# Eight more read buffers in the activations' memory, norm columns read one stage earlier, and another order at the ends of the expert layers

## The chip, the core and the metric

The kernel runs on one core of a Trainium2 chip. The core has five engines that run side by side, each through its own instructions in order: PE (matmuls), DVE (VectorE, element-wise work on 128 partitions), ACT (ScalarE, functions of one input), POOL (GpSimd) and SP, which here only issues transfers. Transfers from the chip's main memory (HBM) to the on-chip memory (SBUF) are asynchronous: an engine issues one, and 16 DMA engines carry it out. Plain reads are issued by SP, reads of rows by an index list (gathers) by POOL. The metric is the time of one execution in microseconds (us); it is the median of several.

## The reference

Two layers, 256 tokens of width 1024, all in float32. With `ada = c @ w_ada + b_ada` split into sh1, sc1, g1, sh2, sc2, g2, each layer computes

```
h      = rmsnorm(x, norm1_g) * (1 + sc1) + sh1
q, k, v, b_gate, c_gate, hc, gate_a, gate_c = split(h @ w_in)
ya     = causal attention(q, k, v) with a distance penalty, 8 heads
yc     = b_gate * short_conv(c_gate * hc)
merged = sigmoid(gate_a) * (ya @ w_attn_proj) + sigmoid(gate_c) * (yc @ w_conv_proj)
x      = x + g1 * (merged @ w_out)
h      = rmsnorm(x, norm2_g) * (1 + sc2) + sh2
q      = h @ w_query; per token and head: top 16 of 128 x 128 pairs of keys, softmax gates
x      = x + g2 * sum over the 8 x 16 chosen experts of gate * gelu(h . expert_u[i]) * expert_v[i]
```

and at the end `rmsnorm(x, final_g)`. There are 16,384 experts in a layer, so expert_u and expert_v have 67 MB each.

## The kernel before

**One stream of reads.** All large weights are read once, in the order of a list named `stream`, in groups of 1 MB (two units of 128 x 1024 floats). `load_ahead` issues the next group on SP as soon as a buffer is free: there are three (`NRAW`) of 8 KB per partition in the pool `strm`, and five others that serve only the first 13 groups. SP issues in order, so a group that waits for a buffer holds up all later ones. `weave(main, extra, spots)` puts extra groups between the weights at given positions. The extra groups are the columns of `ada` (`ada_pair`: a shift and a scale for 128 channels, reduced on DVE in `ada_unit`, line 255) and its rows for the gates (`ada_rows`, line 252).

**Mixer** (the first half of a layer: norm, attention, convolution, gates, output). Its weights are split in a high part (`wh`, ACT, line 305) and a low part (`wl`, DVE or POOL, line 310), and PE multiplies three times. `pol["pool"]` is the share of the low parts that goes to POOL: `POOL_MIX` in most of the mixer, 0.34 in the projections and the output. `unit` prepares units some two to four ahead of the one that PE takes. 16 extra groups go between the weights: eight pairs of columns for the second norm and eight pairs of rows for g1 and g2.

**Expert half.** The two tiles of 128 tokens are treated differently. Tile 0 is *dense*: PE multiplies it with all of expert_u (128 units of 128 experts, line 1052), ACT applies gelu into `halves` (`al` and `ah`, 64 x 128 floats each per partition, the activations), the activations are multiplied by the routing weights that PE builds from one-hot factors (`weigh`, lines 1023 to 1041), and PE multiplies them with all of expert_v (line 1106). Tile 1 is *gathered*: for each of its 128 (head, rank) slots, POOL issues a gather of the 128 chosen rows of expert_u (0.5 MB) and DVE takes a dot product (line 962); the same for expert_v, where DVE adds the scaled row (line 970). So a layer has 128 gathers of each. `NROWS` = 7 gathers can be in flight; `use` consumes the oldest and issues the next.

The order of all this is written out by hand. In the query projection (`query`) scores are handed to `route_all`, a chain of DVE work for the top-k that runs in the background: `fill` takes some of it per step. In the loop over U, each expert unit is followed by one `fill` while routing lasts, or by steps of `weigh` from expert 64 on, and one `use`. In the loop over V, `use` is paced so that the gathers are used up by unit 118 of 128. At unit 122 the update of the gathered tile's `x` is emitted, and after the loop that of the dense tile. In layer 0, eight pairs of columns for layer 1's first norm are woven evenly into U and V. `experts` opens the memory of `al` and `ah` only after the query projection; before that it is the mixer's.

Of the kernel before, what the change touches and what calls it, by code (L numbers as in the profile page):

```python
# [8 lines left out]
F32 = mybir.dt.float32  # L9
# [16 lines left out]
NE = 128  # L26
NROWS = 7
# [5 lines left out]
SPOTS = [int((i + 0.5) * 19 / 16) for i in range(16)]  # L33
# [5 lines left out]
POOL_START, POOL_MIX, POOL_PROJ = 0.5, (0.45, 0.3), 0.34  # L39
# [7 lines left out]
def body(ctx: ExitStack, tc: tile.TileContext, d: dict, out: bass.AP):  # L47
# [60 lines left out]
    for l in range(DEPTH):  # L108
        n = NFIRST[l]
        pairs("qk", d["w_qk"][l, :n], n)  # L110
        pairs("v", d["w_v"][l], 4)
        pairs("qk", d["w_qk"][l, n:], 8 - n)
        pairs("conv", d["w_cv"][l], 12)
        pairs("gate", d["w_gt"][l], 16)
        for u in range(4):
            groups.append(("proj", [(slice(0, 1), d["w_ap"][l][u:u + 1].rearrange("u p c -> p u c")),
                                    (slice(1, 2), d["w_cp"][l][u:u + 1].rearrange("u p c -> p u c"))]))
        a = take_groups()
        ex = [ada_rows(l, r, k) for r in range(2) for k in range(0, KD, 2)]
        if l == 0:  # L120
            cols = [ada_pair(0, 0, m) for m in range(KD)]
            parts = {"c": cols, "u": a[:n // 2], "v": a[n // 2:n // 2 + 2]}
            a = a[n // 2 + 2:]
            start = [parts[ch].pop(0) for ch in START]
            assert not any(parts.values())
            ex = [ada_pair(0, 2, m) for m in range(KD)] + ex
            a = start + weave(a, ex, SPOTS)
        else:
            ex = [ada_pair(l, 2, m) for m in range(KD)] + ex
            a = weave(a, ex, [4 + int(i * 20 / 16) for i in range(16)])  # L130
        stream += a
        pairs("out", d["w_out"][l].rearrange("(k p) c -> k p c", p=128), 8)
# [12 lines left out]
    raws = {}  # L145

# [3 lines left out]
    def load_ahead():  # L150

        while state["dma"] < len(stream):
            kind, parts = stream[state["dma"]]
            if state["dma"] < len(START):
# [166 lines left out]
    def dense_done():  # L321
        raws.pop(state["unit"] // 2)
        state["unit"] += 2
        state["out"] -= 1
        load_ahead()
# [587 lines left out]
    def experts(es, xp, l, hf, pss):  # L913
# [9 lines left out]
        rp = es.enter_context(tc.tile_pool(name="route", bufs=1, side="right"))  # L923
# [86 lines left out]
        ah = es.enter_context(tc.tile_pool(name="acth", bufs=1, side="right")).tile([128, 64, 128], F32, name="ah")  # L1010
        low = ExitStack()
        al = low.enter_context(tc.tile_pool(name="actl", bufs=1, side="right")).tile([128, 64, 128], F32, name="al")
        halves = (al, ah)
# [32 lines left out]
        for e in range(0, NE, 4):  # L1046
# [19 lines left out]
            A.activation(halves[e // 64][:, e % 64:e % 64 + 4], ps, AF.Gelu_apprx_tanh)  # L1066
        for _ in weighing:
            pass
# [6 lines left out]
        for e in range(0, NE, 2):  # L1075
# [14 lines left out]
            if e == 122:  # L1090
                assert not flying and not tasks
                warm_sqrt()
                xg = None
                if fg is not None:
                    xg = tail.tile([128, NT, D], F32, name="xg"), fg
                update(tail, ys, row, 1, xg, 0)
                if xg:
                    z, ops = rstd_ops(1, 2)
                    for op in ops:
                        op()  # L1100
                    scale(xg[0], 1, z, V, A)
            raw = dense("V")
            for x in range(2):
# [6 lines left out]
                while len(tasks) + len(flying) > left * (1 - (i + 1) / 118):  # L1110
# [5 lines left out]
        if xg:  # L1116
            y, ops = rstd_ops(0, 1)
            update(tail, ys, row, 0, xg, 0)
            for op in ops:
                op()  # L1120
            scale(xg[0], 0, y, V, A)
            es.close()
            return None
        pol["pool"] = 1.0
        while len(ready) < 2 and next_unit():
            pass
        update(tail, ys, row, 0, None, 0)
        xps = turn_x((1, 0))
# [12 lines left out]
    for l in range(DEPTH):  # L1141
# [13 lines left out]
        xps = experts(es, xp, l, hf, norm_full(l, xps, hf))  # L1155
# [67 lines left out]
```

## Time and profile before

| | |
|---|---|
| median of 3 runs | 1918.09 us (1917.17 to 1921.28) |
| the profiled execution | 1917.63 us |
| its span, first to last instruction | 1915.8 us |
| busy: PE, DVE | 1637.6 us (85%), 1418.7 us (74%) |
| busy: POOL, ACT | 709.9 us (37%), 572.1 us (30%) |
| moved by transfers | 669.22 MB, 349 GB/s over the span |

The shares are averages over stages with different limits; what holds in one stage is seen only when the span is cut into stages. A busy PE in such a table can still have small gaps, since the ends of matmuls are modelled.

### The profile page before, as it was taken

The numbers are of one execution on the slowest core, as the hardware profiler recorded it, in microseconds if no ns is written. First come the engines' busy times: TensorE is split into PE (matmuls) and PEld (weight loads), VectorE is DVE, ScalarE is ACT, GpSimd is POOL, SyncE is SP. The second block draws the span as 40 slices with busy tenths as digits, with TensorE's granted clock in tenths as the row PEclk, the third lists the DMA queues.
The fourth block names the chain that finished last, engine by engine and source line by source line (L and its number), as shares of the span: only waits on it lengthen the run. The fifth ranks groups of instructions, "written<-read, shape, count | busy, mean of one in ns | idle before, by whom it ended". The sixth has DMA issues, their size and how long they took to land.

```text
span 1915.8 us, 26045 instructions
## 1 busy us (share of the span) xinstructions
PE 1637.6 (85%) x9527; PEld 1273.9 (66%) x9527; DVE 1418.7 (74%) x2996; ACT 572.1 (30%) x1241; POOL 709.9 (37%) x594
## 2 busy tenths in 40 slices
PE   6899998767798979887699999988778998897993
PEld 4789788667798745433258897887777994453331
DVE  7797659999587777755647875699998877777336
ACT  3564421111164423300036444111114553340000
POOL 3423114444244444444232221244444434344223
PEclk7999999997999999998899999999999999998997
DMA  8668459999999999999956784599999999999996
GB/s 317 232 222 314 159 207 398 409 409 379 393 365 393 407 414 410 414 414 413 400 203 238 266 297 144 210 396 409 409 409 409 408 410 389 414 414 401 417 417 244
DMA packets 162961, 669.22 MB, mean 349 GB/s; under 512 B 15761, under 2 KB 15761, under 8 KB 146450
## 3 DMA queue, kind: packets, MB, share of 16 engines
q1 hardware_dynamic: 87106, 396.39, 53.2%
q0 software_dynamic: 73856, 268.48, 35.3%
q10 hardware_dynamic: 1872, 2.69, 0.4%
q8 instruction: 75, 1.23, 0.3%
q14 instruction: 52, 0.43, 0.1%
HBM read 666.46 MB, written 1.05 MB: 348 GB/s over the span
## 4 chain that ended last, share of the span: by engine, by line
DMA 42%; PE 25%; DVE 23%; issue 3%; ACT 2%; POOL 1%; DVEq 0%; SPq 0%; ACTq 0%; POOLq 0%
DMA rows<-in_expert_v_dram,idx 22%; DMA rows<-in_expert_rows_dram,idx 9%; PE mm L1052 8%; DMA raw<-in_expert_u_dram 8%; DVE rows L962 6%; DVE y L970 3%; PE yp L1106 2%; PE mm L897 2%; PE mm L355 2%; PE wp L1039 2%; PE mm L356 2%; PE mm L357 2%; DVE raw L255 1%; DMA raw<-in_w_gt_dram 1%; DMA raw<-in_expert_v_dram 1%
## 5 line engine op out<-in xcount | busy, mean ns | idle before, releaser
L1052 PE MATMUL mm<-hfull,raw 128*128 128x128 f32 x4096 | 514.6, 286 | 109.1 <-DMA raw<-in_expert_u_dram 106.5
L1052 PEld LDWEIGHTS mm<-hfull,raw 128*128 128x128 f32 x4096 | 492.2, 200 | 122.8 <-DMA raw<-in_expert_u_dram 68.7
L970 DVE SCALAR_TENSOR_TENSOR y<-rows,cv,y 128x1024 f32<-128x1024 f32 x254 | 325.7, 1282 | 189.7 <-DMA rows<-in_expert_v_dram,idx 187.0
L946 POOL DMA_INDIRECT rows<-in_expert_rows_dram,idx x256 | 292.0, 1140 | 468.3 <-DVE rows L962 156.2
L946 POOL DMA_INDIRECT rows<-in_expert_v_dram,idx x256 | 282.1, 1102 | 411.5 <-DVE y L970 236.5
L962 DVE SCALAR_TENSOR_TENSOR rows<-rows,h 128x1024 f32<-128x1024 f32 x256 | 308.0, 1217 | 56.9 <-DMA rows<-in_expert_rows_dram,idx 56.5
L1106 PE MATMUL yp<-raw,ah 128*128 128x512 f32 x512 | 244.9, 627 | 47.0 <-DMA raw<-in_expert_v_dram 43.6
L1106 PE MATMUL yp<-raw,al 128*128 128x512 f32 x512 | 246.2, 626 | 17.1 <-DMA raw<-in_expert_v_dram 17.0
L1022 ACT ACTIVATE hp<-iotf,iT 128x128 f32<-128x128 f32 x512 | 162.8, 389 | 230.9 <-PE wp L1039 209.6
L1106 PEld LDWEIGHTS yp<-raw,ah 128*128 128x128 f32 x512 | 97.7, 199 | 192.6 <-issue 106.4
L310 POOL TENSOR_TENSOR wl<-raw,wh 128x1024 fp32r<-128x1024 f32 x43 | 109.8, 2556 | 268.0 <-ACT wh L305 232.6
L1039 PEld LDWEIGHTS wp<-hq,hp 128*128 128x128 f32 x1024 | 131.6, 197 | 67.5 <-issue 67.2
L1106 PEld LDWEIGHTS yp<-raw,al 128*128 128x128 f32 x512 | 96.9, 199 | 119.3 <-issue 100.2
L1039 PE MATMUL wp<-hq,hp 128*128 128x64 f32 x1024 | 134.4, 276 | 30.5 <-DVE hq L1023 30.2
L355 PE MATMUL mm<-hh,wh 128*128 128x256 f32 x512 | 149.2, 291 | 8.8 <-ACT qT L619 4.5
L356 PE MATMUL mm<-hl,wh 128*128 128x256 f32 x512 | 146.1, 285 | 0.0
L357 PE MATMUL mm<-hh,wl 128*128 128x256 f32 x512 | 146.1, 285 | 0.0
L305 ACT ACTIVATE wh<-raw 128x1024 fp32r<-128x1024 f32 x112 | 115.9, 1052 | 86.5 <-DMA raw<-in_w_gt_dram 35.2
L310 DVE TENSOR_TENSOR wl<-raw,wh 128x1024 fp32r<-128x1024 f32 x69 | 104.5, 1524 | 40.6 <-ACT wh L305 40.5
L1023 DVE TENSOR_SCALAR hq<-iotf,jT,gT 128x64 f32<-128x64 f32 x512 | 125.8, 323 | 0.0
L355 PEld LDWEIGHTS mm<-hh,wh 128*128 128x128 f32 x512 | 99.4, 194 | 15.7 <-ACT qT L619 4.7
L255 DVE SCALAR_TENSOR_TENSOR raw<-raw,cbc 128x1024 f32<-128x1024 f32 x64 | 91.1, 1460 | 15.6 <-DMA raw<-in_w_adat_dram 15.6
(218 smaller groups left out, 1922.2 us busy)
## 6 DMA issues: line engine op xcount, KB each, us to landing
raw<-in_expert_u_dram SPq DMA_DIRECT2D x128, 1024.0 KB, 10.9
raw<-in_expert_v_dram SPq DMA_DIRECT2D x128, 1024.0 KB, 8.2
raw<-in_w_adat_dram SPq DMA_DIRECT2D x64, 512.0 KB, 5.7
raw<-in_w_gt_dram SPq DMA_DIRECT2D x16, 1024.0 KB, 5.4
raw<-in_w_adag_dram SPq DMA_DIRECT2D x16, 1024.0 KB, 5.0
raw<-in_w_query_dram SPq DMA_DIRECT2D x16, 1024.0 KB, 4.8
raw<-in_w_cv_dram SPq DMA_DIRECT2D x12, 1024.0 KB, 5.0
raw<-in_w_qk_dram SPq DMA_DIRECT2D x8, 1024.0 KB, 6.2
```

What stands on the lines that cost most here:

```text
L310: l_engine().tensor_tensor(lo, raw, f(h), op=OP.subtract)
L355: T.matmul(ps, h[:, c], mh[:, k], start=first, stop=False)
L356: T.matmul(ps, h[:, c], ml[:, k], start=False, stop=False)
L357: T.matmul(ps, lo[:, c], mh[:, k], start=False, stop=last)
L946: G.indirect_dma_start(out=t, out_offset=None, in_=rows[kind], in_offset=bass.IndirectOffsetOnAxis(ap=idx[:, s:s + 1], axis=0))
L962: V.scalar_tensor_tensor(t, t, 1.0, h1, op0=OP.mult, op1=OP.mult, accum_out=av[:, s:s + 1])
L970: V.scalar_tensor_tensor(y1, t, cv[:, s:s + 1], y1, op0=OP.mult, op1=OP.add)
L1022: A.activation(p[:, i], iotf, AF.Abs, bias=iT[:, t:t + 1])
L1023: V.tensor_scalar(q[:, i], iotf[:, 64 * half:64 * half + 64], jT[:, t:t + 1], gT[:, t:t + 1], op0=OP.is_equal, op1=OP.mult)
L1039: T.matmul(ps[:, t], p[:, t], q[:, t], start=True, stop=True)
L1052: T.matmul(ps[:, u + x], raw[:, x, k * 128:(k + 1) * 128], hf[:, k, :128], start=(k == 0), stop=(k == KD - 1))
L1106: T.matmul(ys[q], halves[i // 64][:, i % 64], raw[:, x, q * 512:(q + 1) * 512], start=(i == 0), stop=(i == NE - 1))
```

## The change

It has three parts. (1) The 64 KB per partition that will hold the activations are opened before the second norm and cut into eight parts of 8 KB (`spare`). Until the activations of a part are written they serve as read buffers: part b may hold a query group or the U groups 0 to 8b + 1. `load_ahead` prefers a spare part over the three old buffers, and `dense_done` gives it back. The pool `route` is opened before them. (2) The eight pairs of columns for layer 1's first norm leave the stream of layer 0's expert half and become the last of the extra groups of layer 0's mixer. `weave` now spreads the extra groups evenly, over the output weights too: 24 among 23 in layer 0, and in layer 1, from the fifth weight group on, 16 among 24 (before: 16 among the first 19, and 16 over 20). `POOL_MIX` goes from (0.45, 0.3) to (0.6, 0.4). (3) In V, the uses are paced so that ten (`LAST`) are left at the end; then the dense tile is updated, the ten are used, and the gathered tile is updated.

```diff
+LAST = 10
-POOL_START, POOL_MIX, POOL_PROJ = 0.5, (0.45, 0.3), 0.34
+POOL_START, POOL_MIX, POOL_PROJ = 0.5, (0.6, 0.4), 0.34
...
-    def weave(main, extra, spots):
+    def weave(main, extra, first=0):
+
         extra = deque(extra)
-        res = []
+        res, n, m = [], len(extra), len(main) - first
         for i, g in enumerate(main):
             res.append(g)
-            if extra and i in spots:
+            while extra and (n - len(extra)) * m < (i + 1 - first) * n:
                 res.append(extra.popleft())
...
+        pairs("out", d["w_out"][l].rearrange("(k p) c -> k p c", p=128), 8)
+        a += take_groups()
+        if l + 1 < DEPTH:
+            ex += [ada_pair(l + 1, 0, m) for m in range(KD)]
+        if l == 0:
+            a = start + weave(a, ex)
+        else:
+            a = weave(a, ex, 4)
...
-        a = take_groups()
-        ex = [ada_pair(l + 1, 0, m) for m in range(KD)] if l + 1 < DEPTH else []
-        stream += weave(a, ex, [int((i + 0.5) * NE / len(ex)) for i in range(len(ex))])
+        stream += take_groups()
...
+    def spare_part(i):
+
+        for b in sorted(spare):
+            if i in place and place[i] <= 8 * b + 1:
+                spare_of[i] = b, spare[b]
+                return spare.pop(b)
+        return None
...
+            elif (t := spare_part(state["dma"])) is not None:
+                pass
             elif state["out"] < NRAW:
...
-            if e == 122:
-                assert not flying and not tasks
                 warm_sqrt()
-                xg = None
-                if fg is not None:
-                    xg = tail.tile([128, NT, D], F32, name="xg"), fg
-                update(tail, ys, row, 1, xg, 0)
...
-                while len(tasks) + len(flying) > left * (1 - (i + 1) / 118):
+                while len(tasks) + len(flying) > LAST + (left - LAST) * (1 - (i + 1) / NE):
...
+        for t in range(NT):
+            while t and flying:
+                use()
+            update(tail, ys, row, t, xg, 1)
...
+        rp = es.enter_context(tc.tile_pool(name="route", bufs=1, side="right"))
+        low = ExitStack()
+        halves = [stack.enter_context(tc.tile_pool(name=f"act{n}", bufs=1, side="right", reuse_waits="tile"))
+                  .tile([128, 64, 128], F32, name=f"a{n}") for n, stack in (("h", es), ("l", low))][::-1]
+        for b in range(8):
+            part = halves[b // 4][:, b % 4 * 16:b % 4 * 16 + 16].rearrange("p j t -> p (j t)")
+            spare[b] = part.rearrange("p (u c) -> p u c", u=2)
+        load_ahead()
+        pss = norm_full(l, xps, hf)
+        xps = experts(es, xp, rp, low, halves, l, hf, pss)
```

## Rows read from the trace of the kernel before

**Rows 1.** The page's part 2: busy tenths and GB/s in 40 equal slices.

```profile
DMA  8668459999999999999956784599999999999996
GB/s 317 232 222 314 159 207 398 409 409 379 393 365 393 407 414 410 414 414 413 400 203 238 266 297 144 210 396 409 409 409 409 408 410 389 414 414 401 417 417 244
```

**Rows 2.** The stretches of the stages; the first line names the columns.

```profile
core 0: us, PE busy (x) PEld busy (x) DVE busy (x) ACT busy (x) POOL busy (x), PEclk, DMA share, GB/s
60.00:217.00 157.00, 151.60 (x1100) 139.31 (x1100) 126.80 (x169) 83.75 (x155) 53.37 (x27) 0.99 0.71 258
177.00:225.00 48.00, 48.00 (x305) 42.98 (x303) 34.58 (x37) 18.88 (x25) 11.56 (x5) 1.00 0.70 258
235.00:275.00 40.00, 38.99 (x202) 34.66 (x201) 17.87 (x71) 6.88 (x16) 2.58 (x3) 1.00 0.39 127
500.00:560.00 60.00, 52.05 (x436) 50.30 (x434) 35.66 (x85) 25.87 (x64) 18.28 (x17) 0.97 0.94 361
645.00:955.00 310.00, 252.59 (x729) 121.72 (x728) 203.32 (x346) 64.12 (x166) 134.59 (x118) 0.93 1.01 411
955.00:980.00 25.00, 23.44 (x56) 10.62 (x56) 6.79 (x8) 3.44 (x6) 2.01 (x1) 0.91 0.82 302
1245.00:1450.00 205.00, 162.89 (x1305) 156.29 (x1305) 193.77 (x537) 31.61 (x45) 89.06 (x80) 0.97 1.02 406
1500.00:1580.00 80.00, 78.51 (x669) 75.59 (x667) 62.33 (x158) 42.95 (x115) 29.61 (x30) 1.00 1.03 410
1885.00:1895.00 10.00, 0.33 (x1) 0.00 (x0) 9.71 (x9) 0.00 (x0) 4.95 (x5) 0.65 0.94 352
```

**Rows 3.** The page's parts 3 and 6: queues (packets, MB), issues (count, KB each).

```profile
q1 hardware_dynamic: 87106, 396.39, 53.2%
q0 software_dynamic: 73856, 268.48, 35.3%
...
raw<-in_expert_u_dram SPq DMA_DIRECT2D x128, 1024.0 KB, 10.9
...
raw<-in_w_adat_dram SPq DMA_DIRECT2D x64, 512.0 KB, 5.7
```

**Rows 4.** Instructions of lines 255 and 310, 60 to 217 us: ns min/median/max.

```profile
L255 DVE SCALAR_TENSOR_TENSOR raw<-raw,cbc x16: 1207/1218/3421, 62.5 to 133.3; 128x1024 f32<-128x1024 f32 x16
...
L310 DVE TENSOR_TENSOR wl<-raw,wh x27: 1211/1226/2469, 61.4 to 216.4; 128x1024 fp32r<-128x1024 f32 x27
...
L310 POOL TENSOR_TENSOR wl<-raw,wh x19: 2360/2456/3055, 62.4 to 211.9; 128x1024 fp32r<-128x1024 f32 x19
```

**Rows 5.** Instructions of line 1052 (U), layers 0 and 1: first and last start.

```profile
L1052 PE MATMUL mm<-hfull,raw x2048: 274/275/582, 296.2 to 645.3; 128*128 128x128 f32 x187
...
L1052 PE MATMUL mm<-hfull,raw x2048: 274/275/553, 1251.9 to 1576.0; 128*128 128x128 f32 x187
```

**Rows 6.** Waits of DVE, 500 to 560 us: total, times, longest.

```profile
DVE raw L255 <- DMA raw<-in_w_adat_dram: 15.6, 1, 15.6
```

**Rows 7.** Timeline of the last 35 us: start, duration, engine, operation.

```profile
1882.47 15.81 DVE L970 SCALAR_TENSOR_TENSOR y<-rows,cv,y 128x1024 f32<-128x1024 f32 x12 [0.31 <-DMA rows<-in_expert_v_dram,idx]
...
1899.11 0.69 DVE L413 TENSOR_TENSOR xt<-xt,tmp 128x512 f32<-128x512 f32 x1
...
1910.39 0.49 DVE L438 TENSOR_SCALAR xg<-xg,ss 128x512 f32<-128x512 f32 x1
```

**Rows 8.** Timeline from 977.9 us, DVE beside POOL.

```profile
977.99 5.12 POOL L310 TENSOR_TENSOR wl<-raw,wh 128x1024 fp32r<-128x1024 f32 x2 [30.56 <-ACT wh L305]
978.64 2.26 DVE L413 TENSOR_TENSOR xt<-xt,tmp 128x512 f32<-128x512 f32 x1
```

**Rows 9.** Line 962 alone (dot products of gathered U rows), routing part: DVE busy.

```profile
1245.00:1450.00 205.00, 73.46 (x122) 0.97 1.02 406
```

**Rows 10.** Line 970 alone (gathered V rows), two stretches: DVE busy.

```profile
1245.00:1450.00 205.00, 22.94 (x18) 0.97 1.02 406
1800.00:1885.00 85.00, 33.33 (x26) 1.00 1.02 416
```

More of the change, by code (lines that the diff above doesn't have):

```diff
@@ L32 @@
 START = "cuuccvcuccvcc"
-SPOTS = [int((i + 0.5) * 19 / 16) for i in range(16)]
 LAGS = (4, 3, 2, 1, 0)
@@ L126, in body @@
             ex = [ada_pair(0, 2, m) for m in range(KD)] + ex
-            a = start + weave(a, ex, SPOTS)
         else:
             ex = [ada_pair(l, 2, m) for m in range(KD)] + ex
-            a = weave(a, ex, [4 + int(i * 20 / 16) for i in range(16)])
+        pairs("out", d["w_out"][l].rearrange("(k p) c -> k p c", p=128), 8)
[6 more added lines that the diff above has]
+            a = weave(a, ex, 4)
         stream += a
-        pairs("out", d["w_out"][l].rearrange("(k p) c -> k p c", p=128), 8)
         pairs("query", d["w_query"][l], 16)
@@ L139, in body @@
                 groups.append((kind, [(slice(0, 2), src[u:u + 2].rearrange("u p c -> p u c"))]))
-        a = take_groups()
-        ex = [ada_pair(l + 1, 0, m) for m in range(KD)] if l + 1 < DEPTH else []
-        stream += weave(a, ex, [int((i + 0.5) * NE / len(ex)) for i in range(len(ex))])
+        stream += take_groups()
     state = {"dma": 0, "unit": 0, "out": 0, "out0": 0, "v": 0}
     raws = {}
+    place = {}
+    for i, g in enumerate(stream):
+        if g[0] == "U":
+            place[i] = place.get(i - 1, -1) + 1
+        elif g[0] == "query":
+            place[i] = -1
+    spare = {}
+    spare_of = {}
+    def spare_part(i):
[4 more added lines that the diff above has]
+        return None
     early = ExitStack()
@@ L321, in dense_done @@
     def dense_done():
-        raws.pop(state["unit"] // 2)
+        g = state["unit"] // 2
+        raws.pop(g)
         state["unit"] += 2
-        state["out"] -= 1
+        if g in spare_of:
+            b, t = spare_of.pop(g)
+            spare[b] = t
+        else:
+            state["out"] -= 1
         load_ahead()
@@ L909, in query, with experts @@
         score(*pend)
-    def experts(es, xp, l, hf, pss):
+    def experts(es, xp, rp, low, halves, l, hf, pss):
         sel = [xp.tile([128, 3, 128], F32, name=f"sel{t}") for t in range(NT)]
@@ L922, in experts @@
         gT = xp.tile([128, 128], F32, name="gT")
-        rp = es.enter_context(tc.tile_pool(name="route", bufs=1, side="right"))
         rows = {"U": d["expert_rows"].rearrange("l e c -> (l e) c"), "V": d["expert_v"].rearrange("l e c -> (l e) c")}
@@ L1009, in experts @@
         hot = hs.enter_context(tc.tile_pool(name="hot", bufs=1))
[L1010 to L1013, printed above, removed]
         def onehots(half, b):
@@ L1066, in experts @@
             A.activation(halves[e // 64][:, e % 64:e % 64 + 4], ps, AF.Gelu_apprx_tanh)
+        spare.clear()
         for _ in weighing:
@@ L1090, in experts @@
             if e == 122:
-                assert not flying and not tasks
                 warm_sqrt()
-                xg = None
-                if fg is not None:
-                    xg = tail.tile([128, NT, D], F32, name="xg"), fg
-                update(tail, ys, row, 1, xg, 0)
[L1097 to L1101, printed above, removed]
             raw = dense("V")
@@ L1115, in experts @@
             dense_done()
[L1116 to L1123, printed above, removed]
-        pol["pool"] = 1.0
[L1125 to L1128, printed above, removed]
+        xg = None
+        if fg is not None:
+            xg = tail.tile([128, NT, D], F32, name="xg"), fg
+        pol["pool"] = 1.0
+        for t in range(NT):
+            while t and flying:
+                use()
+            update(tail, ys, row, t, xg, 1)
+            if xg:
+                y, ops = rstd_ops(t, t + 1)
+                for op in ops:
+                    op()
+                scale(xg[0], t, y, V, A)
+            elif t == 0:
+                while len(ready) < 2 and next_unit():
+                    pass
+        xps = None if xg else turn_x()
         es.close()
@@ L1154, in body @@
         split["stack"].close()
-        xps = experts(es, xp, l, hf, norm_full(l, xps, hf))
+        rp = es.enter_context(tc.tile_pool(name="route", bufs=1, side="right"))
[8 more added lines that the diff above has]
+        xps = experts(es, xp, rp, low, halves, l, hf, pss)
 def lay_out(i):
```

## The prediction

> **What bounds the kernel now.** I read the slices of the span first. The transfer rate has two levels: 365 to 417 GB/s from the 7th of the 40 slices to the 20th and from the 27th to the last but one, and 144 to 317 GB/s in the others [rows 1]. The high stretches are the expert halves of the two layers, the low ones the mixers and the query projections. So I cut the span into stages by hand [rows 2] and asked in each what is full.
>
> Mixer of layer 0 (60 to 217 us): PE busy 151.6 of 157 us, transfers at 258 GB/s; its last third (177 to 225) has PE at 48.0 of 48 and DVE at 34.6. Query phase (235 to 275): PE 39.0 of 40, transfers at 127 GB/s, so two thirds of the transfer rate lie idle. Routing part of an expert half (1245 to 1450): DVE 193.8 of 205 us, and transfers at 406 GB/s; two things are full at once. Rest of the first projection U (1500 to 1580): PE 78.5 of 80, transfers at 410 GB/s. Second projection V (645 to 955): transfers at 411 GB/s, no engine over 82%. End of layer 0 (955 to 980): 302 GB/s and PE 23.4 of 25, because only dense work is left. End of layer 1 (1885 to 1895): PE idle, DVE 9.7 of 10, because only gathered rows are left.
>
> The reader should keep this: in V transfers alone set the end, so a byte moved out of it is worth its transfer time. In U a byte is worth that only if DVE (first part) and PE (second part) have room, and they have 5% and 2%.
>
> The sum is made against the profiled execution, 1917.63 us (span 1915.8 and 1.8 around it); the median of the three runs, 1918.09, is 0.5 us above, which is nothing beside what follows. 0.2%, about 4 us, is what a measurement of this kernel can tell from no change.
>
> **Part one: eight pairs of norm columns leave layer 0's expert half.** A pair is two loads of 512 KB, 1.05 MB in all [rows 3], and two DVE reductions with a median of 1.22 us [rows 4]. Four pairs lie in U and four in V. For U the trace has its own control: layer 1's U is the same program without columns. Its matmuls run from 1251.9 to 1576.0, 324.1 us; layer 0's from 296.2 to 645.3, 349.1 us [rows 5]. The difference is 25.0 us. Four pairs at 406 GB/s are 10.3 us, and DVE once waits 15.6 us for a column that is queued behind U [rows 6], in the stretch where transfers fall to 361 GB/s [rows 2]: together 25.9, which explains it. I take 25. In V, four pairs are 4.2 MB at 411 GB/s, 10 us [rows 2, 3]. Sum of part one: -35 us. In these halves the reductions cost nothing more, since transfers cover them.
>
> **The same columns enter the mixer of layer 0.** There the extra loads go from 16 among 19 weight loads to 24 among 23, and the last eight fall among the projection and output weights. SP gains 16 issues, each of which waits for one of three buffers. Lower bound: nothing, if they fit under PE, since transfers at 258 GB/s have room. Upper bound: each pair lengthens the stage at the rate at which it is fed now, 8 x 1.05 MB / 258 GB/s = 32.5 us. In the last third DVE holds 34.6 of 48 us; 16 reductions add 19.5 and the gate rows that move ahead take some 7 away (six reductions of the same width, an estimate at the columns' 1.22 us), which gives 47 of 48: nearly full, in order, and the weight splits that feed PE queue behind them. Against that, weights are ready some units ahead at the start. I take 8 us, nearer to nothing, because PE is what is full there today.
>
> The larger POOL share (0.45 to 0.6) moves four or five of some 30 splits from DVE (median 1.23 us) to POOL (2.46 us) [rows 4], so some 5.5 us leave DVE and 11 enter POOL, which is at 53 of 157 [rows 2]; I count it as inside the 8. One row speaks against it: an addition that takes 0.69 us elsewhere [rows 7] takes 2.26 us while POOL runs two splits [rows 8]. The Trainium skill, page "SBUF — State Buffer", section "Who interferes with whom", says why that can be: a DVE instruction with two SBUF inputs and a GpSimd instruction that reads SBUF exclude each other, the second waiting until the first has ended. By that rule alone the shift would cost DVE up to 11 us instead of saving 5.5, and the sum would come to about 1891; the trace shows the block, not how often it falls on the path.
>
> Layer 1's mixer gets its 16 extra loads spread over 24 weight loads instead of 20, and more on POOL: I take -2 us, between 0 and -5.
>
> **Part two: eight more read buffers.** Today three buffers let reads run three groups ahead. With the activations' 64 KB per partition as eight more, the query weights are all queued at once and some ten U groups (the first spare part is good only for the first two groups) stand ready when U begins: seven more, 7.3 MB. The query phase has the room: 40 us at 127 GB/s against 406 [rows 2] leave 11 MB. Their issues wait on SP for the mixer's memory, behind query loads already issued, so nothing that PE needs soon stands behind them.
>
> What seven groups are worth per layer: at most 7.3 MB / 406 GB/s = 18 us; at least nothing. I take 5, near the low end, for three reasons from rows. First, in the routing part DVE has only 11 of 205 us idle, so PE's lead can't make that part much shorter. Second, a spare part is given up as U reaches its slice, so at the end of routing (about expert 77) some three groups of the lead are left, and at the end of U none: the lead must be turned into time inside U. Third, the rest of U has PE at 78.5 of 80. Two layers: -10 us.
>
> **Part three: order at the ends.** Before, gathers are paced to end at expert 118 of V and the dense tile's update comes last; after, ten gathers are left when V ends, the dense tile is updated, then the ten are used. In layer 0 transfers at 302 instead of 411 GB/s over 25 us lose 6.6 us; I take -4, since the update (four DVE operations of 0.69 us on the half-rows of one tile, 2.8 us [rows 7]) now stands ahead of the ten uses. If layer 0's end looks like layer 1's once the columns are gone, PE stands idle longer before the next mixer; its granted clock is 0.65 in such a stretch [rows 2]. In layer 1 the last twelve uses already run back to back, 15.8 us for 12, the updates follow at once and the last scaling starts at 1910.39 [rows 7]: DVE is full, and changing the order of its work saves nothing. I take 0 (between -5 and +5).
>
> **Sum.** 1917.6 - 35 + 8 - 2 - 10 - 4 = 1874.6, say 1875 us.
>
> **Rivals.**
>
> *Every byte counts.* If all of U behaves like V, the lead is worth 18 us a layer: 26 us more, 1849. For it: transfers at 406 to 410 GB/s all through U. Against it: DVE and PE just as full there.
>
> *The lead is lost.* PE runs ahead, then stops at the transposes that need routing's result, or the first spare load stands on SP for the mixer's memory until U begins: part two is worth nothing, 1885. For it: DVE's 193.8 of 205.
>
> *The mixer pays the full price.* Layer 0's mixer grows by 32 us instead of 8: 1899. For it: DVE at 47 of 48 by my count.
>
> *Gathers starve, and it ends slower.* One mechanism: the deeper SP queue takes the transfer rate from POOL's gathers while DVE is the bound. In the routing part DVE uses 61 rows of U (122 instructions, two a use) and 18 of V, 79 in 205 us, one per 2.59 us [rows 9, 10]; from 1800 to 1885, with both queues full, 26 in 85 us, one per 3.27 us [rows 10]. If that held through routing in both layers: 158 uses x 0.68 us = 107 us, 1885 + 107 = 1992. It decides once more than some 48 uses are delayed in all (33 us of remaining gain by 0.68). Against it: U's dense stream must wait for DVE's results, so PE's lead and with it the pull are bounded. The Trainium skill, page "DMA: Bandwidth & Descriptors", section "Queues, rings and completion order", says that each engine takes the queues in turn, packet by packet; with 396.39 MB in 87106 packets on SP's queue and 268.48 in 73856 on POOL's [rows 3], 4.55 and 3.64 KB each, gathers would keep 44%, 183 GB/s or 2.87 us per use, and a deeper queue would take no more. The row, 26 x 0.524 MB in 85 us or 160 of 416 GB/s, is a little worse than that [rows 10].
>
> **Chances.** The sum as worked 0.45 (its own range 1862 to 1890); every byte counts 0.18; the lead is lost 0.15; the mixer pays 0.14; parts that cancel to no change 0.03; starving gathers 0.05. The range of 1849 to 1901 leaves out the last two and about half of the case at 1849, 0.17. Faster 0.45 + 0.18 + 0.15 + 0.14 = 0.92, same 0.03, slower 0.05.
>
> **What would show it.** Layer 0's U should take about as long as layer 1's, 315 to 324 us, without a long DVE wait for a column. The query phase should show over 300 GB/s for some 20 us. The mixer of layer 0 should end some 8 us later, with PE waits in its projection and output part. Transfers should fall below 400 GB/s late in routing if the lead is capped; if they stay full and U shrinks by 18 us, the first rival was right. DVE waits for rows in the routing part, near zero now, would show the last. The forecast is wrong if the mixer grows by more than 20 us or U of layer 1 doesn't shrink or shrinks by over 12.

## The result and the profile after

The changed kernel takes 1896.49 us (median of 4 runs, 1895.22 to 1897.50); the kernel before took 1919.61 us beside it, so the ratio is 0.988 (0.9863 to 0.9897). That is some 23 us less, where 43 were forecast. The profiled execution spans 1895.7 us.

The page's transfer rates answer to [rows 1]:

```profile
DMA  8658787999999999999936777699998999999996
GB/s 320 253 209 312 269 315 283 409 409 408 379 349 403 410 416 414 413 416 417 405 137 221 258 284 295 240 394 408 409 408 322 404 407 416 415 415 416 417 415 230
```

The two lowest stretches before layer 0's U have filled (269 and 315 where 159 and 207 stood); the next one falls from 398 to 283, because U begins later. And a hole has come into each layer's U (349 where 365 stood, and 322 where 409 stood). Stage by stage, beside [rows 2]:

```profile
core 0: us, PE busy (x) PEld busy (x) DVE busy (x) ACT busy (x) POOL busy (x), PEclk, DMA share, GB/s
120.00:180.00 60.00, 56.18 (x444) 53.32 (x445) 49.30 (x47) 29.88 (x56) 25.85 (x10) 1.00 0.78 287
180.00:215.00 35.00, 29.46 (x239) 28.68 (x238) 31.36 (x40) 10.09 (x12) 11.29 (x5) 1.00 0.79 278
215.00:250.00 35.00, 29.71 (x112) 21.58 (x111) 29.10 (x43) 11.80 (x18) 4.97 (x2) 0.90 0.77 278
...
265.00:275.00 10.00, 10.00 (x52) 8.92 (x51) 0.00 (x0) 0.77 (x2) 0.00 (x0) 1.00 0.77 299
275.00:320.00 45.00, 44.91 (x234) 40.08 (x233) 35.39 (x130) 9.36 (x20) 12.53 (x12) 1.00 0.64 245
500.00:560.00 60.00, 39.18 (x325) 38.43 (x324) 54.09 (x120) 23.80 (x61) 30.23 (x26) 0.80 0.92 340
650.00:925.00 275.00, 253.14 (x739) 119.33 (x738) 157.33 (x283) 56.33 (x145) 93.70 (x96) 0.98 1.02 415
...
1500.00:1580.00 80.00, 79.86 (x609) 70.70 (x608) 64.52 (x154) 42.72 (x113) 37.21 (x34) 1.00 1.02 409
```

In the mixer of layer 0, PE had no gap in the last third and now has 11 of 70 us free (180 to 250 us), beside DVE at 60 of 70. Its waits there (177 to 250 us: total, times, longest) are for weight splits and gates:

```profile
PE yp L812 <- DVE wl L332: 3.2, 2, 2.4
PE yp L812 <- POOL wl L332: 2.2, 2, 1.9
PE yp L811 <- ACT wh L327: 2.2, 2, 1.5
PE mm L382 <- DVE gt L785: 2.2, 1, 2.2
```

Work that PE waits for has become late. U's products answer to [rows 5], first and last start:

```profile
L1074 PE MATMUL mm<-hfull,raw x1024: 274/275/582, 330.6 to 639.2; 128*128 128x128 f32 x171
...
L1074 PE MATMUL mm<-hfull,ah x832: 274/275/582, 319.9 to 600.8; 128*128 128x128 f32 x167
```

U of layer 0 runs from 319.9 to 639.2, 319 us instead of 349. It also starts 23.7 us later than the 296.2 of before. So 30 us are gained in this U and 24 lost ahead of it; most of the rest is 5 us each from layer 0's V and layer 1's U and V.

The table cuts every kernel in this text into the same stages (us), in one profiled execution each. A mixer runs from its first projection product to the first query product, U from its first product to the end of its last, V from there to the end of the last update or of the kernel. Left out are the query projection, 55.4 us, which differs in two kernels only, where the text says so, the start up to the first mixer (64.9 to 67.4 us, 2.5 us longer after than before), and some 26 us between the layers. Ratios are to the kernel before on the same chip, with intervals of about 0.002 to either side.

| kernel | ratio | mixer 0 | U, layer 0 | V, layer 0, to last update | mixer 1 | U, layer 1 | V, layer 1, to end |
|---|---|---|---|---|---|---|---|
| before | 1 | 175.9 | 349.4 | 338.1 | 187.4 | 324.3 | 339.6 |
| after | 0.9880 | 197.1 | 319.5 | 333.6 | 187.6 | 319.1 | 334.6 |
| e1_columns_back | 0.9936 | 184.3 | 331.9 | 340.3 | 187.2 | 318.9 | 334.6 |
| e2_no_spare | 1.0047 | 197.5 | 329.8 | 335.4 | 192.4 | 323.7 | 339.2 |
| e3_narrow_columns | 0.9868 | 193.2 | 320.3 | 332.5 | 188.0 | 319.5 | 336.2 |
| e4_four_buffers | 0.9830 | 192.8 | 315.2 | 333.7 | 186.8 | 316.2 | 332.4 |
| e5_mix_back | 0.9867 | 191.7 | 319.0 | 333.3 | 186.1 | 317.8 | 334.5 |
| e6_end_order | 0.9901 | 201.9 | 319.6 | 331.5 | 186.5 | 319.1 | 334.7 |
| e7_columns_in_query | 0.9930 | 185.8 | 328.4 | 334.9 | 187.1 | 319.2 | 334.8 |
| e8_spare_alone | 0.9847 | 171.7 | 331.8 | 338.9 | 186.8 | 319.6 | 332.7 |
| e9_query_spread_end | 0.9896 | 181.7 | 329.0 | 330.7 | 189.1 | 319.3 | 333.9 |
| e10_pace | 0.9944 | 203.1 | 318.1 | 336.3 | 187.5 | 318.8 | 338.5 |
| e11_four_mix_pace | 0.9758 | 186.7 | 317.5 | 328.6 | 184.2 | 316.7 | 332.5 |
| e11_four_narrow | 0.9770 | 180.4 | 316.8 | 333.2 | 186.9 | 316.8 | 331.4 |

One caution: after, e2, e6 and e10 run the same program in mixer 0, and took 197.1, 197.5, 201.9 and 203.1 us (before and e8, also of one program there, 175.9 and 171.7). A difference of one mixer by less than some 6 us says little.

### The profile page after: what moved, and what is told of

Its sections match the earlier page's. It is cut to its first block, busy times and chain, and to the rows that moved or that the text cites. A ratio compares the mean times of both kernels' runs of the same rounds, so it can differ in the third digit from the quotient of the medians.

```text
span 1895.7 us, 26021 instructions
## 1 busy us (share of the span) xinstructions
PE 1613.9 (85%) x9524; PEld 1262.2 (67%) x9527; DVE 1435.7 (76%) x2987; ACT 571.1 (30%) x1241; POOL 708.4 (37%) x603
## 4 chain that ended last, share of the span: by engine, by line
DMA 38%; DVE 29%; PE 20%; issue 5%; ACT 2%; POOL 2%; DVEq 0%; POOLq 0%; ACTq 0%; SPq 0%
DMA rows<-in_expert_v_dram,idx 21%; DMA rows<-in_expert_rows_dram,idx 13%; PE mm L1074 8%; DVE y L996 6%; DVE rows L988 5%; PE wp L1061 3%; DVE raw L277 2%; PE mm L924 2%; DVE wl L332 2%; PE mm L382 1%; PE mm L383 1%; PE mm L384 1%; POOL rows L972 1%; DVE ti L824 1%; DVE sc L825 1%
## 5 line engine op out<-in xcount | busy, mean ns | idle before, releaser
L972 POOL DMA_INDIRECT rows<-in_expert_rows_dram,idx x256 | 274.0, 1070 | 490.3 <-DVE rows L988 155.9
L972 POOL DMA_INDIRECT rows<-in_expert_v_dram,idx x256 | 273.5, 1068 | 393.0 <-DVE y L996 237.0
L1074 PE MATMUL mm<-hfull,raw 128*128 128x128 f32 x2048 | 247.9, 281 | 24.9 <-ACT al L1088 24.9
L1074 PEld LDWEIGHTS mm<-hfull,raw 128*128 128x128 f32 x2048 | 240.0, 196 | 25.6 <-ACT al L1088 25.6
L1119 PE MATMUL yp<-raw,al 128*128 128x512 f32 x512 | 233.9, 600 | 0.3 <-DMA raw<-in_expert_v_dram 0.2
L332 POOL TENSOR_TENSOR wl<-raw,wh 128x1024 fp32r<-128x1024 f32 x52 | 135.2, 2605 | 249.0 <-ACT wh L327 231.5
L1074 PE MATMUL mm<-hfull,ah 128*128 128x128 f32 x1664 | 203.6, 285 | 17.6 <-ACT ah L1088 9.2
L1074 PEld LDWEIGHTS mm<-hfull,ah 128*128 128x128 f32 x1664 | 199.4, 201 | 18.4 <-ACT ah L1088 9.6
L1061 PEld LDWEIGHTS wp<-hq,hp 128*128 128x128 f32 x1024 | 129.6, 196 | 65.1 <-issue 64.9
L1119 PEld LDWEIGHTS yp<-raw,al 128*128 128x128 f32 x512 | 92.4, 190 | 94.2 <-issue 92.1
L327 ACT ACTIVATE wh<-raw 128x1024 fp32r<-128x1024 f32 x112 | 116.0, 1052 | 101.9 <-DMA raw<-in_w_gt_dram 37.2
L332 DVE TENSOR_TENSOR wl<-raw,wh 128x1024 fp32r<-128x1024 f32 x60 | 91.7, 1538 | 35.4 <-ACT wh L327 35.1
```

The lines of the kernel that those rows point to most:

```text
L332: l_engine().tensor_tensor(lo, raw, f(h), op=OP.subtract)
L972: G.indirect_dma_start(out=t, out_offset=None, in_=rows[kind], in_offset=bass.IndirectOffsetOnAxis(ap=idx[:, s:s + 1], axis=0))
L1061: T.matmul(ps[:, t], p[:, t], q[:, t], start=True, stop=True)
L1074: T.matmul(ps[:, u + x], raw[:, x, k * 128:(k + 1) * 128], hf[:, k, :128], start=(k == 0), stop=(k == KD - 1))
L1119: T.matmul(ys[q], halves[i // 64][:, i % 64], raw[:, x, q * 512:(q + 1) * 512], start=(i == 0), stop=(i == NE - 1))
```

## The experiments

All but e8 start from the changed kernel.

**The columns back in the experts (e1).** The norm columns stand between U and V reads again; the rest of the change stays.

```diff
-        if l + 1 < DEPTH:
-            ex += [ada_pair(l + 1, 0, m) for m in range(KD)]
...
-        stream += take_groups()
+        a = take_groups()
+        if l + 1 < DEPTH:
+            ex = [ada_pair(l + 1, 0, m) for m in range(KD)]
+            spots = {int((i + 0.5) * NE / KD): g for i, g in enumerate(ex)}
+            a = [y for i, g in enumerate(a) for y in ([g, spots[i]] if i in spots else [g])]
+        stream += a
...
```

> The changed kernel with the eight column pairs of layer 1's first norm back in layer 0's expert half, every 16th group as before; the other parts stay. If a stage costs what the traces show, layer 0's query projection begins some 22 us earlier (242 instead of 264.5 us), layer 0's U takes some 25 us longer (344 instead of 319.5) and its V 5 to 10 longer: about 1905 us, between 1900 and 1912. Rival: the columns in the mixer cost nothing that the mixer wouldn't pay anyway (the larger POOL share or the spread extra loads are what lengthens it): then the query projection still begins after 255 us, and the time is 1920 or more.

1903.12 us beside 1915.46, ratio 0.9936 (0.9915 to 0.9956), against 0.988 for the change: about 11 us by the ratios, 5 by the spans. The seven runs of this kernel lie between 1896.08 and 1908.90, wider than any other's, so its one profile (1902.36) is a weaker witness than the others. By the stages, moving the columns is worth this little because it takes 12.4 us out of U and 6.7 out of V and puts 12.8 into the mixer.

**Without the eight buffers (e2).** The list of spare parts stays empty, so only the three old buffers read.

```diff
-            spare[b] = part.rearrange("p (u c) -> p u c", u=2)
+            part.rearrange("p (u c) -> p u c", u=2)
```

> The changed kernel without the eight read buffers: the activations' memory is opened early, but no read goes into it. If the lead of seven groups is worth 5 us a layer because DVE bounds routing and PE the rest of U, layer 1's U takes 324 us again (319 with the buffers) and the time is 1905 to 1909. If every byte read early counts: 18 us a layer, 1932. If the lead is lost whole: 1896.

1923.26 beside 1915.46, ratio 1.0047 (1.003 to 1.0064). The rest of the change, without the buffers, makes the kernel slower by some 8 us; the buffers are worth 32 us by the ratios and 25 by the spans, 10.3 of it in U of layer 0 and 4.6 in U of layer 1.

**The buffers alone (e8).** The kernel before with only the spare parts added to it.

```diff
...
+            elif (t := spare_part(state["dma"])) is not None:
+                pass
...
+        for b in range(8):
+            part = halves[b // 4][:, b % 4 * 16:b % 4 * 16 + 16].rearrange("p j t -> p (j t)")
+            spare[b] = part.rearrange("p (u c) -> p u c", u=2)
+        load_ahead()
...
```

> The kernel before with the eight read buffers and nothing else of the change: the columns stay in the first layer's U and V, the shares, the order at the ends and the pacing are the old ones. If the buffers are worth what taking them out of the changed kernel cost (25 us by the spans, 32 us by the medians), about 1885 to 1890 us where the kernel before takes about 1915, with the first layer's U near 339 us and the second's near 319. If they are worth the 10 us of the forecast, about 1905 us. If every byte counts, 36 us, about 1879. If the columns' leaving the experts is what lets the buffers work (the two depend on each other), the first layer's U stays within 5 us of 349.

1886.01 beside 1916.31, ratio 0.9847 (0.9829 to 0.9866): 29 us, and on its own better than the whole change. U of layer 0 falls by 17.6 us although its columns stay. DVE's longest waits in 296 to 650 us show why; the kernel before had one of 15.6 us for a column there [rows 6]:

```profile
DVE al L1059 <- PE wp L1057: 17.4, 30, 3.4
DVE y L992 <- DMA rows<-in_expert_v_dram,idx: 12.5, 10, 2.4
DVE gT L885 <- PE wp L883: 0.4, 1, 0.4
```

The wait for a column is gone, and only the buffers differ. So the forecast's two parts were not independent: the buffers alone take away the stall that part one was credited with. The rest of the gain is seen in PE's waits. Before, for the first and the second layer's U:

```profile
PE mm L1052 <- DMA raw<-in_expert_u_dram: 60.8, 32, 6.2
...
PE mm L1052 <- DMA raw<-in_expert_u_dram: 45.7, 39, 2.5
```

With the buffers alone, in the first layer and then in the second:

```profile
PE mm L1070 <- DMA ah<-in_expert_u_dram: 20.8, 13, 6.2
...
PE mm L1070 <- DMA raw<-in_expert_u_dram: 12.1, 11, 2.1
PE mm L1070 <- ACT al L1084: 10.9, 2, 6.9
...
PE mm L1070 <- ACT al L1084: 23.4, 4, 9.2
PE wp L883 <- DVE sel L861: 13.3, 2, 10.8
```

PE waited for U's reads 60.8 and 45.7 us. With the buffers 34 us of this are left in layer 0 and none in layer 1, where new waits behind routing (37 us) take the place of most of them: ACT, whose results PE needs, stands in its turn behind a routing step that waits for DVE (1245 to 1500 us).

```profile
ACT sel L846 <- DVE sel L845: 81.3, 6, 19.4
```

In layer 1 U is only 4.7 us shorter, but V and the end another 6.9. V's transfers now start full (the first 40 us of V ran at 384 GB/s before and at 415 now, worth 3 us), and two more gathered rows have been used by then (37 instead of 35, 2 x 0.524 MB, 2.6 us). So a lead can pay in the next stage, if that stage is bound by bytes.

**Narrow reductions (e3).** The second layer's columns are reduced over 128 of the 1024 elements of each row, which changes what these columns hold; reads stay as they are.

```diff
-        V.scalar_tensor_tensor(raw, raw, 1.0, cbc, op0=OP.mult, op1=OP.mult, accum_out=col)
+        w = slice(0, 128 if (l, r) == (1, 0) else D)
+        V.scalar_tensor_tensor(raw[:, w], raw[:, w], 1.0, cbc[:, w], op0=OP.mult, op1=OP.mult, accum_out=col)
```

> The changed kernel with the DVE reductions of layer 1's first norm columns over 128 of their 1024 elements; every load stays, and so the norm of layer 1 is scaled by other columns than the reference's. If DVE's work in the mixer (62 of 72 us in its last third) is what lengthens it by 24 us, layer 0's query projection begins 12 to 20 us earlier and the time is 1876 to 1885. If the three buffers feed the mixer no faster than 265 GB/s whatever DVE does, it begins within 4 us of 264.5 and the time is 1892 to 1897.

**Four read buffers instead of three (e4).** Room for the fourth comes from one buffer less for the first 13 groups and for three tiles of the mixer (`p`, `pt`, `yc`).

```diff
-NRAW, NRAW0 = 3, 5
+NRAW, NRAW0 = 4, 4
...
-            p = pool.tile([128, 384], F32, name="p", bufs=5)
+            p = pool.tile([128, 384], F32, name="p", bufs=4)
...
```

> The changed kernel with four read buffers of the stream instead of three; to make room the first 13 groups have four buffers instead of five, and three tiles of attention and convolution one buffer less. If the number of buffers sets the mixer's feed, layer 0's query projection begins 10 us or more earlier, counted from the first projection of the mixer (67.4 to 264.5 us, 197 us, in the changed kernel), and layer 1's mixer is a little shorter too: some 1880 us. If DVE's work sets it: under 4 us, 1891 to 1900.

**Both (e11_four_narrow).** Again the columns of the second layer hold something else.

> The changed kernel with four read buffers and, besides, the reductions of the second layer's norm columns over 128 of the 1024 elements of each row (this changes what those columns hold; the transfers stay as they are). Either edit alone took 4 us out of the first mixer (193 us instead of 197). If VectorE and the number of buffers bound that mixer in turn, so that each hides the other's gain, the two together bring it below 185 us. If the transfers themselves bound it, it stays at 189 to 194 us, and the whole at about 1880 us.

e3: 1889.65 beside 1915.46, 0.9868 (0.9851 to 0.9884); mixer 0 193.2 us. e4: 1881.59, 0.983 (0.9814 to 0.9846); mixer 192.8, with both U and the last V 2 to 4 us shorter too. Either alone takes 4 us out of the mixer, which is within the 6 us of the caution above. Both: 1870.43 beside 1916.31, 0.977 (0.9749 to 0.9791), and the mixer falls to 180.4 us, 17 less. Its windows, beside the stretches from 180 us on of the changed kernel above:

```profile
180.00:215.00 35.00, 35.00 (x257) 33.36 (x256) 29.50 (x59) 13.97 (x18) 9.66 (x5) 1.00 0.95 360
215.00:240.00 25.00, 24.16 (x111) 17.71 (x112) 15.41 (x37) 11.75 (x25) 4.20 (x2) 1.00 0.99 375
```

PE is full again, and transfers run at 360 GB/s where they ran at 278. So the reads themselves were not the limit in this mixer. DVE's time and the few buffers are, in turn, since the two edits together give twice what they give apart. With three buffers a read cannot be issued until DVE, which works in order, has come to the reduction that frees one; half of SP's waits in the changed kernel (177 to 215 us) are of this kind:

```profile
SPq L187 <- DVE acol L280: 7.2, 1, 7.2
...
SPq L187 <- DVE raw L277: 4.7, 1, 4.7
...
SPq L187 <- DVE adac L279: 3.1, 2, 1.5
```

With four, the reductions' own length is next.

**The old shares of POOL (e5).**

```diff
-POOL_START, POOL_MIX, POOL_PROJ = 0.5, (0.6, 0.4), 0.34
+POOL_START, POOL_MIX, POOL_PROJ = 0.5, (0.45, 0.3), 0.34
```

> The changed kernel with POOL's share of the low parts in the mixers back at 0.45 and 0.3. In the changed kernel layer 0's mixer takes 197.1 us from its first projection to the first query product, 175.9 before the change. If the larger share helps DVE, the mixer grows by some 5 us and the time is up by as much; if it hurts, because POOL's splits and DVE's operations with two inputs block each other, the mixer shrinks by 5 to 11 us. If the feed of reads sets the stage, with DVE's work and three buffers both part of it, it stays within 3 us.

1887.11 beside 1913.69, 0.9867 (0.9851 to 0.9884): 2.5 us less than the change by the ratios, too little for the measurement to tell; mixer 0 falls by 5.4, also within the caution. The groups of instructions by line and shape, 60 to 250 us, say more (busy us, mean ns of one). Before:

```profile
L310 DVE TENSOR_TENSOR wl<-raw,wh 128x1024 fp32r<-128x1024 f32 x27 | 38.5, 1436 | 15.8 <-ACT wh L305 15.7
L255 DVE SCALAR_TENSOR_TENSOR raw<-raw,cbc 128x1024 f32<-128x1024 f32 x16 | 23.6, 1510 | 0.0
```

After:

```profile
L277 DVE SCALAR_TENSOR_TENSOR raw<-raw,cbc 128x1024 f32<-128x1024 f32 x32 | 56.1, 1787 | 1.9 <-DMA raw<-in_w_adat_dram 1.9
L332 DVE TENSOR_TENSOR wl<-raw,wh 128x1024 fp32r<-128x1024 f32 x22 | 30.7, 1403 | 8.4 <-ACT wh L327 8.1 <-ACT p L684 0.3
```

And with the old shares:

```profile
L277 DVE SCALAR_TENSOR_TENSOR raw<-raw,cbc 128x1024 f32<-128x1024 f32 x32 | 45.6, 1463 | 1.5 <-DMA raw<-in_w_adat_dram 1.5
L332 DVE TENSOR_TENSOR wl<-raw,wh 128x1024 fp32r<-128x1024 f32 x27 | 38.7, 1443 | 15.0 <-ACT wh L327 15.0
```

A reduction has a median of 1.22 us, but a mean of 1.79 beside the larger POOL share and 1.46 beside the smaller. The 16 more of them cost DVE 32.5 us (56.1 - 23.6), not the 19.5 of the forecast. The larger share takes 8.0 us of splits from DVE (38.7 - 30.7) and adds 10.5 to its reductions (56.1 - 45.6): a loss of 2.5. Besides, a split takes POOL 2.6 us and DVE 1.4. The Trainium skill, page "SBUF — State Buffer", section "Who interferes with whom", says that a DVE instruction with two SBUF inputs and a POOL instruction that reads SBUF exclude each other: the 10.5 us agree with it, and lie near the up to 11 us that the prediction estimated by it. The share alone does not set the mean, though: in e11_four_mix_pace, with the same 19 splits on POOL and a shorter mixer than the changed kernel's, it is 1.68 us.

**The columns among the query reads (e7), and there with the old spread and the next mixer's first splits behind the last gathers (e9).** The forecast saw 11 MB of room in the query phase; here the columns' reads are put there instead of in the mixer. In e9 the output weights also carry no extra loads in layer 0, and the end has the order of e6 below.

```diff
-        if l + 1 < DEPTH:
-            ex += [ada_pair(l + 1, 0, m) for m in range(KD)]
...
-        stream += take_groups()
+        a = take_groups()
+        if l + 1 < DEPTH:
+            ex = [ada_pair(l + 1, 0, m) for m in range(KD)]
+            a = a[:1] + ex[:2] + a[1:2] + ex[2:4] + a[2:3] + ex[4:6] + a[3:4] + ex[6:] + a[4:]
+        stream += a
```

> The changed kernel with the eight column pairs neither in the mixer nor in V and U, but between the first four query groups, where DVE waits 20 us for its first scores and transfers have room left. If the mixer's 21 us are paid for the columns and for the spread of the extra loads over the output weights, the first part comes back: mixer 184 us as with the columns in the expert half, U of layer 0 some 320 us as in the changed kernel, and the time is 12 to 14 us under the changed kernel's. Rival: the reductions delay routing, which is DVE's, by up to 21 us, and U of layer 0 grows by as much: no gain.

> The same place for the columns, and also the 16 remaining extra loads of layer 0's mixer again ahead of its output weights, and the next mixer's first splits behind the last ten uses. If each is worth what the stages show: mixer 176 to 180 us, U of layer 0 320, end of layer 0's expert half 40 instead of 45.9: some 25 us under the changed kernel, 1866 to 1874 where the kernel before takes 1915. Rival: the mixer's 8 us come from the larger POOL share, not from the spread: mixer 184, 18 us under the changed kernel.

e7: 1900.48 beside 1913.69, 0.993 (0.9913 to 0.9946); e9: 1893.96, 0.9896 (0.988 to 0.9913). The mixer falls to 185.8 and 181.7, but the query projection takes 64.2 and 62.8 us instead of 55.4, and U 328.4 and 329.0 instead of 319.5. A window of e7 in the query phase:

```profile
265.00:285.00 20.00, 13.04 (x64) 11.43 (x63) 18.27 (x65) 2.33 (x6) 0.00 (x0) 0.88 0.68 256
```

DVE is full (18.3 of 20): six reductions take 7.1 us of it, most of the rest is routing. PE stands still for 7 us, and not for DVE: it waits for one query read, which SP issues late, since SP itself waits 12.9 us for a buffer that a reduction frees (250 to 320 us):

```profile
PE mm L926 <- DMA al<-in_w_query_dram: 7.0, 1, 7.0
...
SPq L189 <- DVE adac L281: 14.3, 2, 12.9
```

Later, in U, PE never waits for a read; its waits behind routing come to 55.9 us, where the changed kernel has 49.1. Room in the transfer rate was not room on DVE. Nothing is gained over the mixer: the rival in e7's expectation, reductions that delay routing, came true in both.

**The splits after the last gathers (e6).** At the end of layer 0 the next mixer's first weight splits, which POOL runs ahead of the last three gathers, come behind the uses.

```diff
+            if t and not xg:
+                while len(ready) < 2 and next_unit():
+                    pass
...
-            elif t == 0:
-                while len(ready) < 2 and next_unit():
-                    pass
```

> The changed kernel with one step moved at the end of layer 0's expert half: the first weight splits of the next mixer are prepared behind the last ten uses of gathered rows and not ahead of them. In the changed kernel POOL works 6.2 us on two splits while the last three gathers wait behind them in its order, and seven uses take 13.1 us instead of 9.2. If that is lost time, the stretch from V's last product to the end of the update shrinks from 45.9 to 38 to 41 us and the time falls by 5 to 7 us. If the splits then come too late for the next norm's products, nothing is gained: within 2 us.

1895.14 beside 1913.69, 0.9901 (0.9884 to 0.9917): no gain. V of layer 0 with its last update is 2.1 us shorter, less than the mixers of one program differ.

**Uses paced over 106 experts instead of 128 (e10).**

```diff
-                while len(tasks) + len(flying) > LAST + (left - LAST) * (1 - (i + 1) / NE):
+                while len(tasks) + len(flying) > max(LAST, left * (1 - (i + 1) / 106)):
```

> The changed kernel with the vector uses of V handed out over the first 106 of its 128 experts, instead of 128, down to the same last ten. Theory of the two queues: plain reads and gathers share the memory, and in the last third of V the plain reads win, so that a tail with gathers alone is left (46 us at 294 GB/s in the first layer, 48 us in the second). Uses taken sooner move gathers ahead into V: dense V longer by 5 to 10 us, the tails shorter by 12 to 20 us, the whole 8 to 20 us shorter. Rival: the tail is set by VectorE's updates and the last products and not by the gathers; then the tails shrink by what V grows, and the whole stays within 4 us of the changed kernel.

1905.62 beside 1916.31, 0.9944 (0.9927 to 0.9961). The theory of the tail falls. After V's last product the changed kernel works 46 us in layer 0 with gathers and hardly any products, and that looked like time to be won:

```profile
927.00:950.00 23.00, 0.18 (x2) 0.02 (x1) 16.77 (x15) 0.04 (x1) 12.28 (x13) 0.61 1.01 390
950.00:973.00 23.00, 3.30 (x12) 2.42 (x14) 20.51 (x16) 4.03 (x8) 10.73 (x6) 0.50 0.52 198
```

With the earlier pacing, the corresponding stretch:

```profile
925.00:950.00 25.00, 23.23 (x52) 9.16 (x50) 3.37 (x3) 0.30 (x2) 2.81 (x3) 1.00 1.02 417
950.00:978.00 28.00, 6.13 (x21) 3.29 (x22) 21.96 (x18) 4.06 (x8) 9.99 (x5) 0.63 0.54 197
```

The tail is 24 us instead of 46, and dense V grew by all of it (312.0 instead of 287.7). The first half of the tail already moved 390 GB/s; only its last 23 us, the dense update, ten uses and the other update, run at half rate, and these remain. That the whole is slower than the change, by 8.4 us in the spans and 12 by the ratios, is not explained by the pacing alone: 6.0 of it lie in mixer 0, whose program is the same, 2.7 and 3.9 in the two V stages.

**Four buffers, the old shares, and this pacing (e11_four_mix_pace).** The edits of e4, e5 and e10 together.

> The changed kernel with four read buffers instead of three (four instead of five in the first mixer, and fewer buffers for p, pt and yc), the old shares of GpSimd in the mixers, and the uses paced over 106 experts. If the three edits add up as measured or expected apart (-10, -3, -8 to -15 us), 1868 to 1876 us beside a kernel before of about 1915. If the pacing gives nothing, 1880 to 1885.

1870.59 beside 1916.31, 0.9758 (0.9742 to 0.9775), the fastest of the kernels that compute the reference: 2.4% under the kernel before. Against e4 it gains 6.1 us in mixer 0, no more than one program's mixers differ, and 5.1 in V of layer 0.

## Why the prediction came out as it did

The sign and the range held; 1875 us were forecast and 1896 measured, a little more than half of the forecast gain. By its own last sentence, though, the forecast is wrong: the mixer of layer 0 grew by 21.2 us, more than the 20 that it allowed. The spans differ by 20.1 us (1915.8 to 1895.7), and the stages say where the forecast's terms went:

| step | forecast | measured, and where |
|---|---|---|
| columns leave U | -25 | -19.6 without the buffers (before to e2), -12.4 with them (e1 to after) |
| columns leave V, and the end of layer 0 | -14 | -4.5 (before to after) |
| mixer 0: columns, shares, spread | +8 | +21.2 (before to after) |
| mixer 1 | -2 | +0.2 |
| eight buffers | -10 | by the spans -31 alone (e8), -25 within the change (e2) |
| end of layer 1, with V | 0 | -5.0, most of it the buffers' (e8: -6.9) |

The step that failed most is the mixer's, "I take 8 us, nearer to nothing, because PE is what is full there today". It is mis-sized by 13 us and the rival of the full price (32 us) lies nearer. By the table, the columns are worth 11 to 13 of it (after against e7 and e1); the larger share and the finer spread together make up the rest: e1 has both without the columns and stands 12.6 us above e8. What each is worth is not shown: e5 and e9, each without one of them, are 5.4 and (beside e7) 4.1 us better, less than one program's mixers differ. Two things were wrong in the reasoning. The DVE time of a reduction was taken from the median, 1.22 us, though the maximum in the same row was 3421 ns [rows 4]; in the changed mixer the mean is 1.79. And the 32.5 us bound was priced by the rate of transfer, while what limited the stage was buffers that DVE frees: the rate rises to 360 GB/s once both are eased (e11_four_narrow).

The second is the buffers' worth. "I take 5, near the low end" a layer rested on engines that are full in U. The rate was the thing to look at over the whole expert half, U and V: with the buffers alone (before to e8) 11.6 us came out of layer 1's (663.9 to 652.3) and 16.8 out of layer 0's (687.5 to 670.7), against the bound of 18. "Every byte counts", with 36 us for both, was nearly right about the buffers. The reasons given against it were true, and did not decide: PE does stop for routing (13.8 and 23.4 us in layer 0 of the changed kernel), and transfers do fall, to 340 GB/s in 500 to 560 us:

```profile
PE mm L1074 <- ACT al L1088: 23.4, 4, 10.9
PE wp L887 <- DVE sel L865: 13.8, 2, 11.3
```

But the 60.8 and 45.7 us that PE had waited for reads stand in no row of the forecast. They were the room; the new waits behind routing took most of it, and the rest, with what it brought in V, was more than twice the 5 us.

Third, the 25 us of part one were split nearly rightly (10.3 us of bytes and a stall of 15.6): with the stall gone and the columns still there, in e8, U of layer 0 is 12.2 us longer than layer 1's. But the forecast missed that part two takes the stall away too, so that one gain was counted for part one which either part brings. In U the two errors, too much for the columns and too little for the buffers, nearly cancel (30 us forecast in layer 0 and 29.9 measured), and that is luck; the mixer's 13 us and the V term's 10 are what is left.

Right in the forecast: U of layer 0 as long as layer 1's (319.5 and 319.1 us), no wait for a column, the dip late in routing. The query phase is half right: 299 GB/s in 265 to 275 us and 245 in 275 to 320, against 127 before, where over 300 for some 20 us was forecast. The gathers do not starve: DVE waits 9.3 us for U's rows in layer 0's U and 3.6 in layer 1's (0 and 8.3 before). The lead is not lost.

Open: why U of layer 0 in e2, which has neither the columns nor the buffers, is still 6.1 us longer than layer 1's; how the part of the mixer's growth that is not the columns divides between shares and spread, since one program's mixer differs by 6 us from one kernel to another; and why layer 0's V with its end gave 4.5 us back and not 14. By the stages, the columns' leaving is 6.7 of it (e1 to after), where 10 were forecast, and the new order at the end, which was to gain 4, costs 1.4 (e8 to e1); in layer 1 it costs 1.9. Differences this small between single profiles are a hint and no more; with the last 23 us at half rate they would make part three's -4 us wrong in sign.

## What to carry to other kernels

Price an instruction that another engine's work can stretch by its mean in the stretch where it will run, not by its median; and where reads are issued only as an engine frees buffers, count that engine's queue, not the spare transfer rate. Before a lookahead is called small, sum PE's waits for those reads, as an upper bound, and follow the lead past its stage. Try the parts of a change alone: here one part brought 29 us, the rest together cost about 6.

## What the runs showed of the hardware

A reduction with two SBUF inputs, 1.22 us by its median, stretched from a mean of 1.46 to 1.79 us as POOL took 24 instead of 19 splits; moving elementwise work to POOL cost DVE 2.5 us more in its reductions than it saved in splits. And a PE left almost idle (3.3 of 23 us busy, 950 to 973 us) had a granted clock of 0.50, its lower level of 1.2 GHz: four transposes that begin at 971.8 us take 1.11 us there:

```profile
971.79 1.11 PE L405 MATMUL mm<-ident,xt 128*128 128x128 f32 x4 [19.30 <-DVE xt L440]
```

In e10, where PE had just worked and the granted clock was 1.00 (954.4 to 955.2 us), the same four take 0.66 us:

```profile
954.50 0.66 PE L405 MATMUL mm<-ident,xt 128*128 128x128 f32 x4 [0.71 <-DVE xt L440]
```

The next mixer was no longer for that stretch, 187.6 us against 187.4 before.
